# Hybrid encoder, two layers on one core: a bias table stored per query, and a gated product written row-major

## Chip, core and metric

The kernel runs on one core of a Trainium2 chip. The metric is device time in microseconds (us) of one execution, taken as the median of the runs.

## What is computed

Two layers of a bidirectional encoder over 512 tokens of width 1024, all float32. Layer 0 mixes with eight latent-attention heads (MLA) and eight 2-D neighbourhood heads, layer 1 with retention and Hyena; behind each mixer stands a gated convolutional feed-forward block. Every sub-layer is `x = x + rms_norm(f(rms_norm(x)))`. What the change touches:

```python
def neighbourhood_attention(q, k, v, rpb):      # 8 rows x 64 columns of tokens, window 8 x 16
    ...
        row_off = rs + jnp.arange(kh) - r + (NA_WIN_H - 1)
        bias = jnp.transpose(rpb[:, row_off][:, :, col_off], (0, 2, 1, 3))
        s = (jnp.einsum('bchd,bicjhd->bhcij', q_row, k_win).astype(jnp.float32) * scale
             + bias.astype(jnp.float32)[None])
    ...
def conv_ffn(h, w_gate, w_up, conv_w, w_down):
    g = dwconv3(h @ w_gate, conv_w)
    return (jax.nn.gelu(g, approximate=True) * (h @ w_up)) @ w_down
```

## The kernel before

Activations lie transposed: eight tiles of 128 features x 512 tokens. Each float32 product is made of three TensorE products of rounded halves (`mm`, L278: hi x hi, lo x hi, hi x lo, one line each, L280 to L282). Weights come in pieces of 512 KB through SyncE's queue (`load_weight`, L250): DMA into one of two `raw` tiles, ScalarE (ACT) writes `whi` (L259), VectorE (DVE) writes `wlo` (L260), four pairs of them. The order of each engine's instructions is fixed when the program is built: a scheduler with its own costs takes the code's order, with a few priorities (`high_priority`) and pins (`issue_after`).

Layer 0 and its feed-forward block hold the tokens column-major: token position = column x 8 + row. The table of biases `rpb` (8 heads, 15 x 31 offsets) is loaded by eight DMAs of short rows into `rpbraw` (L568 to L570). In `na0` (L626) TensorE multiplies, for each head, a 128 x 128 permutation (`perm`, loaded behind the mask) by a strided view of that head's slice, 384 columns in float32 (L633), which leaves the biases of 128 queries in PSUM; DVE adds three windows of it to the mask (L637). `na1` takes scores and softmax (L655, L658, L666, L671), `na2` transposes and multiplies by the values. The latent projections run between the heads, the MLA heads follow (`ml0` to `ml2`).

In `ffn(l)` (L875) each of 22 steps projects gate (`psA`) and up (`pspj`), convolves and gates; the product (L911) is written over `g` and split into `ahi` and `alo`. `prod(k)` multiplies these by the down weights, 66 matmuls for each of eight output tiles. The block's output is to be row-major (position = row x 64 + column) for layer 1. `boundary` (L339) does this with `perm=True`: the first seven output tiles are multiplied column-major, and the evacuation from PSUM (`evac`, L355 to L364) reads them by the view `rc`. The last one (`late`) is done in two halves of 256 tokens, each 66 matmuls, whose moving operand is read by `rc`: every eighth float, 32 bytes apart. After the first half come its norm (`stats` L292, L297, L299) and, pinned behind 18 matmuls of the second half, `spread` (L316); then `update` on DVE (L395, L396, L334) makes the next block's `h`, and `squares` (L409, L410) runs on ACT and GpSimd (POOL). `proj_halves` is the first work of the next block on it. The feed-forward block of layer 1 has the same code without `rc`.

Of the kernel before, what the change touches and what calls it, by code (L numbers as in the profile page):

```python
# [10 lines left out]
F32 = mybir.dt.float32  # L11
# [5 lines left out]
P = 128  # L17
S = 512
# [25 lines left out]
def shape_constants():  # L44

    c = {}
    tok0 = (np.arange(S) % GR) * GW + np.arange(S) // GR

    def rope(dim):
        inv = np.float32(10000.0) ** (-np.arange(0, dim, 2, dtype=np.float32) / np.float32(dim))  # L50
        ang = np.arange(S, dtype=np.float32)[:, None] * inv.astype(np.float32)[None, :]
        return np.cos(ang).astype(np.float32), np.sin(ang).astype(np.float32)

    co, si = rope(32)
    co, si = co[tok0].T, si[tok0].T
    cc, ss = np.concatenate([co, co]), np.concatenate([-si, si])
    qs = np.float32(MSCALE)
    c["rope0"] = f32(np.stack([np.concatenate([np.full((64, S), qs), cc * qs, ss * qs]),
                               np.concatenate([ss, ss, cc, cc])], 1).reshape(P, 2 * S))
    co, si = rope(128)  # L60
    co, si = co.T, si.T
    c["rope1"] = f32(np.stack([np.concatenate([co, co]), np.concatenate([-si, si])], 1).reshape(P, 2 * S))

    mask = np.zeros((P, 3, 32, GR), np.float32)
    for typ, (q0, k0) in enumerate(((0, 0), (16, 8), (48, 32))):
        for p in range(P):
            col = q0 + p // GR
            st = min(max(col - 8, 0), GW - 16)
            kc = k0 + np.arange(32)
            mask[p, typ, (kc < st) | (kc >= st + 16), :] = -1.0e30  # L70
    perm = np.zeros((P, P), np.float32)
    q = np.arange(P)
    perm[(7 - q % 8) * 16 + 15 - q // 8, q] = 1.0
    c["namask"] = f32(np.concatenate([mask.reshape(P, 3 * 256), perm], 1))

    c["dist"] = f32(np.arange(896)[None, :] - 384 - np.arange(P)[:, None])

    t = np.arange(S, dtype=np.float32) / np.float32(S - 1)
    w = np.float32(2.0 * math.pi) * np.arange(S, dtype=np.float32) / np.float32(S)
    f = np.linspace(1e-4, 15, 16, dtype=np.float32)  # L80
    fw = f[None, :] * w[:, None]
    c["fz"] = f32(np.concatenate([t[:, None], np.cos(fw), -np.sin(fw)], 1).T)
    dl = np.linspace(math.log(1e-2) / 1.5, math.log(1e-2) / 0.3, HC, dtype=np.float32)
    win = np.exp(-t[:, None] * np.abs(dl)[None, :]).astype(np.float32)
    wb = win.copy()
    wb[0] = 0.0
    perm = np.concatenate([np.arange(0, S, 2), np.arange(1, S, 2)])
    c["fwin"] = f32(np.stack([win[perm], wb[perm]]).reshape(2, 4, P, HC).transpose(2, 1, 0, 3).reshape(P, 8 * HC))

    k = np.arange(256)  # L90
    th = (2 * k + 1) * PI / 1024
    mats = []
    for par in (0, 1):
        tt = np.arange(par, S, 2)
        mats += [np.cos(tt[:, None] * th[None, :]), np.sin(tt[:, None] * th[None, :])]
    fwd = f32(np.stack([m.reshape(2, P, 256) for m in mats]))
    inv = f32(np.stack([m.T.reshape(2, P, 256) for m in mats]))
    for name, m in (("dftf", fwd), ("dfti", inv)):
        m = f32(m.transpose(2, 0, 1, 3).reshape(P, 4 * 512))
        hi = rounded(m)  # L100
        c[name] = f32(np.concatenate([hi, m - hi], 1))
    return c
# [13 lines left out]
def lay_out(inp):  # L116
# [75 lines left out]
    ffn(1)  # L192
    a["w"] = f32(np.stack(pieces))

    r = np.transpose(inp["a_rpb"][0], (1, 0, 2))
    a["rpb"] = f32(np.pad(r, ((0, 0), (0, 0), (16, 16))))
    fw = np.zeros((P, 64 + 64 + 64 + 1024), np.float32)
    fw[:33, 0:64] = inp["c_filt_w1"][0]
    fw[:64, 64:128] = inp["c_filt_w2"][0]
# [6 lines left out]
class Body:  # L206
# [132 lines left out]
    def boundary(self, pool, tag, x, prod, gpost, gpre, ns, ftag, perm=False, rin=None):  # L339
# [8 lines left out]
        def evac(k, ps, cs, full):  # L348
            n = cs.stop - cs.start
            f = fs[k][:, cs]  # L350
            src = ps
            if perm and full:
                src, f = rc(ps), v3(f)
            if k == 0:
                nc.scalar.activation(v3(acc[:, cs]) if perm and full else acc[:, cs], src, AF.Square)  # L355
            else:
                sq = new("sq")[:, :n]
                with ExitStack() if full else self.tc.high_priority(HP):
                    nc.scalar.activation(v3(sq) if perm and full else sq, src, AF.Square)
                    if k < KT - 1 or cs.start == 0:  # L360
                        nc.vector.tensor_tensor(acc[:, cs], acc[:, cs], sq, ALU.add)
                    else:
                        lastsq.append(sq)
            nc.scalar.activation(f, src, AF.Copy, scale=self.col(gpost + k))  # L364

        for k in range(KT - ns):
            fs.append(self.X("f", tag=ftag))
# [190 lines left out]

    def mixer0(self, p, h, acc):
        nc = self.nc  # L560
        mask = p.tile([P, 3 * 256 + P], F32, name="namask")
        perm = mask[:, 768:]
        rope = p.tile([P, 2, S], F32, name="rope0")
        rpb = self.I["rpb"]
        big = p.tile([P, 8, 8, 48], F32, tag="big", name="rpbraw")

        def loads():
            for r in range(8):  # L568
                src = bass.AP(rpb.tensor, rpb.offset + r * 504, [[1, 16], [63, 64], [1, 48]])
                nc.sync.dma_start(big[16 * r:16 * r + 16].rearrange("p a b c -> p (a b) c"), src)  # L570
            nc.sync.dma_start(mask, self.I["namask"])
            nc.sync.dma_start(rope, self.I["rope0"].rearrange("p (a b) -> p a b", a=2))
        ebuf = []
        for i in range(4):
# [51 lines left out]
        def na0(hd, _):  # L626
            if hd % 2 == 0:
                q = qk_tile(self.proj(h))
                kn = self.X("kn", tag="xb")
                nc.vector.tensor_tensor(kn, self.proj(h), Rb, ALU.mult)  # L630
                pair[hd // 2] = q, qk_tile(kn)
            ps = self.PS("B")
            nc.tensor.matmul(ps[:, :384], perm, big[:, :, hd].rearrange("p r c -> p c r"), start=True, stop=True)  # L633
            b = p.tile([P, 2, 256], F32, tag="bias", bufs=2, name=self.nm("bias"))
            b = [b[:, 0], b[:, 1], self.X("bias", tag="xb")[:, :256]]
            for t, o in enumerate((128, 64, 0)):
                nc.vector.tensor_tensor(b[t], ps[:, o:o + 256], mask[:, t * 256:t * 256 + 256], ALU.add)  # L637
            return b

        def na1(hd, bias):  # L640
# [234 lines left out]
    def ffn(self, p, x, h, pre, l):  # L875
# [20 lines left out]
        for j in range(FT):  # L896
            if j % 2 == 0:
                next(steps, None)
            gps, ups = pre[2 * j:2 * j + 2] if j < 2 else (self.proj(h, "A"), self.proj(h, "pj"))
            cw = [self.col(C_FC + l * 66 + t * 22 + j) for t in range(3)]  # L900
            t, g = self.X("t"), self.X("g")
            nc.vector.tensor_tensor(t, gps, Rb, ALU.mult)  # L902
            nc.scalar.activation(g, t, AF.Copy, scale=cw[1])
            nc.vector.scalar_tensor_tensor(g[:, sh:], t[:, :S - sh], cw[0], g[:, sh:], ALU.mult, ALU.add)
            nc.vector.scalar_tensor_tensor(g[:, :S - sh], t[:, sh:], cw[2], g[:, :S - sh], ALU.mult, ALU.add)
            if l == 0:
                nc.vector.scalar_tensor_tensor(g[:, 1:8], t[:, 504:511], cw[0], g[:, 1:8], ALU.mult, ALU.add)
                nc.vector.scalar_tensor_tensor(g[:, 504:511], t[:, 1:8], cw[2], g[:, 504:511], ALU.mult, ALU.add)
            nc.scalar.activation(g, g, AF.Gelu_apprx_tanh)

            nc.vector.tensor_tensor(g, ups, g, ALU.mult)  # L911
            hi = p.tile([P, S], F32R, name=f"ahi{l}_{j}")
            lo = p.tile([P, S], F32R, name=f"alo{l}_{j}")
            self.split_to(hi, lo, g)
            a.append((hi, lo))
        rc = lambda t: t.rearrange("p (c r) -> p r c", r=GR)

        def prod(k, late=False):
            w = [self.weight() for _ in range(3)]

            def run(ps, cut):
                for q in range(FT):
                    self.mm(ps, self.wslice(w[q // 8], slice(q % 8 * P, q % 8 * P + P)), (cut(a[q][0]), cut(a[q][1])),
                            q == 0, q == FT - 1)
                    if q in (YQ, FT - 1):
                        yield ps
            if not late:
                return list(run(self.PS("pj"), lambda t: t))[-1]
            if l == 0:
                return lambda cs: run(self.PS("A")[:, :256], lambda t: rc(t)[:, cs.start // GW:cs.stop // GW])  # L930
            return lambda cs: run(self.PS("A")[:, :256], lambda t: t[:, cs])
        return self.boundary(p, "s", x, prod, C_FPOST + 8 * l, C_MPRE + 8 if l == 0 else None, 1, "xa", perm=(l == 0), rin=rcol)


# [338 lines left out]
```

## Time and profile before

| | |
|---|---|
| median of 3 runs | 1348.27 us (1347.58 to 1350.19) |
| profiled execution, its own time | 1350.83 us |
| its span, first to last instruction | 1349.1 us |
| PE (TensorE matmul) busy | 1308.6 us, 97% |
| PEld (weight load) busy | 1079.5 us, 80% |
| DVE / ACT / POOL busy | 812.9 / 571.4 / 149.8 us (60 / 42 / 11%) |
| mean granted clock of TensorE | 0.985 |

Busy times overlap, and matmuls are pipelined: the distance from one start to the next says what one costs, its duration says more than that. An engine's idle time costs only where another one waits for it. The stages lie in the span as follows: neighbourhood heads with latent projections to about 143 us, MLA heads to about 240 us, first feed-forward block from about 310 us, its down products from 536 us, its last output tile from 642.55 us, layer 1 from about 700 us. A clock of 1.0 is TensorE's full one, 0.5 the half.

### The profile page before, as it was taken

To read this page: it belongs to the slowest core of one execution; us is meant where nothing else is said; L and a number is where in the kernel's file an instruction comes from. 1 tells how busy PE (TensorE), PEld (TensorE's weight loads), DVE (VectorE), ACT (ScalarE), POOL (GpSimd) and SP (SyncE) were. 2 spreads that over 40 slices of the span, in tenths; PEclk is the share of its full clock that TensorE was granted. 3 is DMA by queue.
4 is the path that set the end of the run, shared out by engine and by line. 5 is a ranking of instruction groups with operands and counts; after the bars stand their busy time and mean duration, and the time that the engine had idled before them with its cause. 6 is when DMAs were issued, how large, how long until landed. Compare 5 with 4: busy or idle time off the path is not lost. (4 is left out here: it accounts for less than half of the span.)

```text
span 1349.1 us, 16493 instructions
## 1 busy us (share of the span) xinstructions
PE 1308.6 (97%) x6386; PEld 1079.5 (80%) x6386; DVE 812.9 (60%) x1276; ACT 571.4 (42%) x925; POOL 149.8 (11%) x138
## 2 busy tenths in 40 slices
PE   9999899999999999999987999999999999999997
PEld 8777677897877788888986878777988888888886
DVE  7577898388755555222387796785676555552223
ACT  5346699456533333222254333333654333333221
POOL 4011232040001000000050000222120000000002
PEclk9999899999999999999998999999999999999998
DMA  7811001324334323333235222212323333233331
GB/s 194 146 67 63 16 24 57 93 67 132 109 125 141 109 94 94 109 101 103 63 131 181 79 94 93 90 50 66 123 79 111 103 99 94 94 95 108 109 95 63
DMA packets 49146, 130.42 MB, mean 97 GB/s; under 512 B 12875, under 2 KB 15115, under 8 KB 48556
## 3 DMA queue, kind: packets, MB, share of 16 engines
q1 hardware_dynamic: 43452, 116.72, 28.5%
q10 hardware_dynamic: 5040, 8.45, 1.9%
q0 software_dynamic: 576, 4.19, 0.8%
q8 instruction: 50, 0.82, 0.2%
q14 instruction: 28, 0.23, 0.1%
HBM read 123.06 MB, written 6.29 MB: 96 GB/s over the span
## 5 line engine op out<-in xcount | busy, mean ns | idle before, releaser
L259 ACT CAST whi<-raw 128x1024 fp32r<-128x1024 f32 (+1 forms) x200 | 209.1, 1047 | 422.7 <-PE pspj L281 224.1
L260 DVE TENSOR_TENSOR wlo<-raw,whi 128x1024 fp32r<-128x1024 f32 (+1 forms) x200 | 247.3, 1239 | 206.5 <-ACT whi L259 202.4
L280 PE MATMUL pspj<-h,whi 128*128 128x512 f32 (+1 forms) x664 | 252.0, 380 | 0.1
L281 PE MATMUL pspj<-h,whi 128*128 128x512 f32 (+1 forms) x664 | 250.4, 377 | 1.4 <-DVE h L334 1.4
L282 PE MATMUL pspj<-h,wlo 128*128 128x512 f32 (+1 forms) x664 | 249.9, 376 | 0.1
L282 PE MATMUL psA<-h,wlo 128*128 128x512 f32 (+1 forms) x424 | 156.6, 370 | 4.4 <-DVE wlo L260 4.3
L280 PE MATMUL psA<-h,whi 128*128 128x512 f32 (+1 forms) x424 | 157.9, 372 | 0.0
L281 PE MATMUL psA<-h,whi 128*128 128x512 f32 (+1 forms) x424 | 156.1, 368 | 0.0
L281 PEld LDWEIGHTS pspj<-h,whi 128*128 128x128 f32 x664 | 126.1, 190 | 24.4 <-DVE h L334 1.8
L280 PEld LDWEIGHTS pspj<-h,whi 128*128 128x128 f32 x664 | 126.0, 190 | 22.9 <-issue 0.4
L282 PEld LDWEIGHTS pspj<-h,wlo 128*128 128x128 f32 x664 | 125.8, 189 | 22.9 <-DVE wlo L260 0.5
L280 PE MATMUL pspj<-ahi,whi 128*128 128x512 f32 x308 | 121.4, 394 | 0.0
L282 PE MATMUL pspj<-ahi,wlo 128*128 128x512 f32 x308 | 120.7, 392 | 0.0
L281 PE MATMUL pspj<-alo,whi 128*128 128x512 f32 x308 | 119.5, 388 | 0.0
L280 PEld LDWEIGHTS psA<-h,whi 128*128 128x128 f32 x424 | 80.9, 191 | 19.8 <-issue 4.6
L282 PEld LDWEIGHTS psA<-h,wlo 128*128 128x128 f32 x424 | 80.9, 191 | 19.5 <-DVE wlo L260 6.3
L281 PEld LDWEIGHTS psA<-h,whi 128*128 128x128 f32 x424 | 80.9, 191 | 12.6
L299 POOL TENSOR_TENSOR r<-v,mhalf 128x2 f32<-128x2 f32 (+1 forms) x14 | 14.3, 1019 | 636.4 <-DVE v L297 540.7
L902 DVE TENSOR_TENSOR t<-psA,Rb 128x512 f32<-128x512 f32 x40 | 27.6, 691 | 90.5 <-PE psA L282 90.5
L911 DVE TENSOR_TENSOR g<-pspj,g 128x512 f32<-128x512 f32 x40 | 27.6, 691 | 69.8 <-PE pspj L282 63.4
L282 PEld LDWEIGHTS pspj<-ahi,wlo 128*128 128x128 f32 x308 | 57.8, 188 | 13.5
L281 PEld LDWEIGHTS pspj<-alo,whi 128*128 128x128 f32 x308 | 57.8, 188 | 12.9
(351 smaller groups left out, 2265.0 us busy)
## 6 DMA issues: line engine op xcount, KB each, us to landing
raw<-in_w SPq DMA_DIRECT2D x198, 512.0 KB, 3.5
x<-in_xT SPq DMA_DIRECT2D x16, 256.0 KB, 4.6
fc<-in_fwin SPq DMA_DIRECT2D x8, 256.0 KB, 3.4
filt<-fa SPq DMA_DIRECT2D x8, 256.0 KB, 2.0
xspill<-f ACTq DMA_DIRECT2D x8, 256.0 KB, 2.2
sd<-filt ACTq DMA_DIRECT2D x8, 256.0 KB, 3.4
x<-xspill ACTq DMA_DIRECT2D x8, 256.0 KB, 2.9
rpbraw<-in_rpb SPq DMA_DIRECT2D x8, 192.0 KB, 7.9
```

The costliest lines, as they stand in the source:

```text
L259: nc.scalar.copy(hi[:, c], raw[:, c])
L260: nc.vector.tensor_tensor(lo[:, c], raw[:, c], hi[:, c].bitcast(F32), ALU.subtract)
L280: nc.tensor.matmul(ps, stat[0], mov[0], start=start, stop=False)
L281: nc.tensor.matmul(ps, stat[0], mov[1], start=False, stop=False)
L282: self.last_mm = nc.tensor.matmul(ps, stat[1], mov[0], start=False, stop=stop).ins
L299: self.pow = nc.gpsimd.tensor_tensor(r, v, self.mhalf[:, :c], ALU.pow)
L902: nc.vector.tensor_tensor(t, gps, Rb, ALU.mult)
L911: nc.vector.tensor_tensor(g, ups, g, ALU.mult)
```

## The change

Two parts. The bias table is laid out ahead of the run, per query: partition q holds, for each head, the 384 biases that the permutation product made; eight DMAs become four with rows of 3072 bytes, the matmul goes, and DVE adds from SBUF instead of PSUM. In the first feed-forward block DVE writes the gated product row-major into `t` (whose last reader is done), from contiguous reads with writes 256 bytes apart; all down products then read contiguously, and PSUM is evacuated without a permuted view.

```diff
-    perm = np.zeros((P, P), np.float32)
-    q = np.arange(P)
-    perm[(7 - q % 8) * 16 + 15 - q // 8, q] = 1.0
-    c["namask"] = f32(np.concatenate([mask.reshape(P, 3 * 256), perm], 1))
+    c["namask"] = f32(mask.reshape(P, 3 * 256))
...
-    r = np.transpose(inp["a_rpb"][0], (1, 0, 2))
-    a["rpb"] = f32(np.pad(r, ((0, 0), (0, 0), (16, 16))))
+    r = np.pad(inp["a_rpb"][0], ((0, 0), (0, 0), (16, 16)))
+    q = np.arange(P)
+    r = r[:, 7 - (q % GR)[:, None, None] + np.arange(GR)[None, None, :], 15 - (q // GR)[:, None, None] + np.arange(48)[None, :, None]]
+    a["rpb"] = f32(r.transpose(1, 0, 2, 3).reshape(P, MH * 384))
...
-            src = ps
-            if perm and full:
-                src, f = rc(ps), v3(f)
...
-            nc.scalar.activation(f, src, AF.Copy, scale=self.col(gpost + k))
+            nc.scalar.activation(f, ps, AF.Copy, scale=self.col(gpost + k))
...
-        big = p.tile([P, 8, 8, 48], F32, tag="big", name="rpbraw")
+        big = p.tile([P, MH, 384], F32, tag="big", name="rpb")
 
         def loads():
-            for r in range(8):
-                src = bass.AP(rpb.tensor, rpb.offset + r * 504, [[1, 16], [63, 64], [1, 48]])
-                nc.sync.dma_start(big[16 * r:16 * r + 16].rearrange("p a b c -> p (a b) c"), src)
             nc.sync.dma_start(mask, self.I["namask"])
+            for hd in range(0, MH, 2):
+                nc.sync.dma_start(big[:, hd:hd + 2], self.I["rpb"][:, hd * 384:hd * 384 + 768].rearrange("p (a b) -> p a b", a=2))
...
-            ps = self.PS("B")
-            nc.tensor.matmul(ps[:, :384], perm, big[:, :, hd].rearrange("p r c -> p c r"), start=True, stop=True)
...
-                nc.vector.tensor_tensor(b[t], ps[:, o:o + 256], mask[:, t * 256:t * 256 + 256], ALU.add)
+                nc.vector.tensor_tensor(b[t], big[:, hd, o:o + 256], mask[:, t * 256:t * 256 + 256], ALU.add)
...
-            nc.vector.tensor_tensor(g, ups, g, ALU.mult)
+            if l == 0:
+                cr = lambda a: a.rearrange("p (c r) -> p c r", r=GR)
+                nc.vector.tensor_tensor(t.rearrange("p (r c) -> p c r", c=GW), cr(ups), cr(g), ALU.mult)
+                g = t
+            else:
+                nc.vector.tensor_tensor(g, ups, g, ALU.mult)
...
-                return list(run(self.PS("pj"), lambda t: t))[-1]
-            if l == 0:
-                return lambda cs: run(self.PS("A")[:, :256], lambda t: rc(t)[:, cs.start // GW:cs.stop // GW])
-            return lambda cs: run(self.PS("A")[:, :256], lambda t: t[:, cs])
+                return list(run(self.PS("pj"), slice(0, S)))[-1]
+            return lambda cs: run(self.PS("A")[:, :256], cs)
```

The scheduler sets another order in layer 0's mixer; from the MLA heads on the order is the same on every engine. On TensorE, before, the permutation products of heads 0 to 2 stood between the scores of head 1 (`psA_579`) and the next pair's projection (`pspj_535`):

```order
## PE: 6202 rows
187 L280 MATMUL psA_579<-qkh_446,qkh_409 128x256
188 L281 MATMUL psA_579<-qkl_447,qkh_409 128x256
189 L282 MATMUL psA_579<-qkh_446,qkl_410 128x256
190 L633 MATMUL psB_450<-rpbraw,namask 128x384
191 L633 MATMUL psB_457<-rpbraw,namask 128x384
192 L633 MATMUL psB_571<-rpbraw,namask 128x384
193 L280 MATMUL pspj_535<-h_147,whi_380 128x512
194 L281 MATMUL pspj_535<-h_148,whi_380 128x512
195 L282 MATMUL pspj_535<-h_147,wlo_381 128x512
```

With the change one projection of the second pair follows the other directly at this place:

```order
## PE: 6193 rows
181 L280 MATMUL pspj_491<-h_161,whi_315 128x512
182 L281 MATMUL pspj_491<-h_162,whi_315 128x512
183 L282 MATMUL pspj_491<-h_161,wlo_316 128x512
184 L280 MATMUL pspj_527<-h_147,whi_376 128x512
185 L281 MATMUL pspj_527<-h_148,whi_376 128x512
186 L282 MATMUL pspj_527<-h_147,wlo_377 128x512
```

The eight permutation products are gone from TensorE, and head 1's scores stand after the second projection. On DVE, before, the first biases (L637) stood behind the first two pairs' `qkl` and ahead of the first scores (`s_472`):

```order
## DVE: 1260 rows
31 L630 TENSOR_TENSOR kn_413<-pspj_414,Rb_217 128x512
32 L275 TENSOR_TENSOR qkl_447<-kn_413,qkh_446 128x512
33 L275 TENSOR_TENSOR qkl_531<-pspj_499,qkh_530 128x512
34 L637 TENSOR_TENSOR bias_452<-psB_450,namask 128x256 x2
35 L637 TENSOR_TENSOR bias_453<-psB_450,namask 128x256
36 L655 SCALAR_TENSOR_TENSOR s_472<-psA_465,rn,bias_452 128x256
```

With the change four of them (L629) stand ahead of the statistics of the first norm (`v_299`, L295), and behind the last weight split ahead of it:

```order
## DVE: 1260 rows
17 L260 TENSOR_TENSOR wlo_143<-raw_141,whi_142 128x1024
18 L629 TENSOR_TENSOR bias_446<-rpb,namask 128x256 x2
19 L629 TENSOR_TENSOR bias_451<-rpb,namask 128x256 x2
20 L295 TENSOR_SCALAR v_299<-psB_294 128x4
...
39 L275 TENSOR_TENSOR qkl_443<-kn_409,qkh_442 128x512
40 L647 SCALAR_TENSOR_TENSOR s_464<-psA_457,rn,bias_446 128x256 x2
```

The first scores (`s_464`, L647) are then formed before the second pair's `qkl`, and the first biases wait for the mask and the first piece of the table alone.

## Rows read from the trace of the kernel before

**Rows 1.** Page, busy time and share of the span by engine, then instructions.

```profile
PE 1308.6 (97%) x6386; PEld 1079.5 (80%) x6386; DVE 812.9 (60%) x1276; ACT 571.4 (42%) x925; POOL 149.8 (11%) x138
```

**Rows 2.** Busy us (instructions) by stretch; at the end clock, DMA share, GB/s.

```profile
54.00:143.00 89.00, 88.22 (x441) 68.41 (x440) 70.38 (x146) 45.89 (x104) 12.70 (x10) 0.98 0.24 77
143.00:160.00 17.00, 13.48 (x54) 10.23 (x54) 13.78 (x30) 11.33 (x31) 6.17 (x6) 0.70 0.00 1
330.00:535.00 205.00, 205.00 (x873) 161.97 (x872) 122.67 (x187) 76.28 (x95) 10.16 (x8) 1.00 0.35 111
```

**Rows 3.** PE's timeline, permutation products: start, us, what; two passes per product.

```profile
51.02 4.33 PE L633 MATMUL psB<-rpbraw,namask 128*128 128x384 f32 x6
54.57 1.02 PE L280 MATMUL pspj<-h,whi 128*128 128x512 f32 x1
...
76.30 1.52 PE L633 MATMUL psB<-rpbraw,namask 128*128 128x384 f32 x2
77.75 0.38 PE L280 MATMUL psA<-qkh,qkh 64*128 64x256 f32 x1
...
132.94 1.46 PE L633 MATMUL psB<-rpbraw,namask 128*128 128x384 f32 x2
134.23 0.29 PE L677 MATMUL psB<-ident,s 128*128 128x128 f32 x1
```

**Rows 4.** PE's timeline, late products of the first feed-forward block, then its norm.

```profile
642.55 0.38 PE L280 MATMUL psA<-ahi,whi 128*128 128x256 f32 x1
...
658.44 0.40 PE L281 MATMUL psA<-alo,whi 128*128 128x256 f32 x1
658.65 0.74 PE L292 MATMUL psB<-ones,acc 128*128 128x1 f32 x6
...
661.49 0.40 PE L316 MATMUL psC<-ident,r 128*128 128x128 f32 x2
```

**Rows 5.** The same of the second feed-forward block.

```profile
1321.84 0.28 PE L280 MATMUL psA<-ahi,whi 128*128 128x256 f32 x1
...
1330.44 0.28 PE L281 MATMUL psA<-alo,whi 128*128 128x256 f32 x1
1330.71 0.83 PE L292 MATMUL psB<-ones,acc 128*128 128x1 f32 x6
...
1332.66 0.38 PE L316 MATMUL psC<-ident,r 128*128 128x128 f32 x2
```

**Rows 6.** DVE's timeline behind the first late half; in brackets idle before, releaser.

```profile
657.54 0.42 DVE L361 TENSOR_TENSOR acc<-acc,sq 128x256 f32<-128x256 f32 x1 [12.11 <-ACT sq L359]
...
661.92 0.75 DVE L395 TENSOR_TENSOR f<-f,psC 128x256 f32<-128x256 f32 x2 [2.55 <-PE psC L316]
...
665.23 0.48 DVE L334 SCALAR_TENSOR_TENSOR h<-f,cols,h 128x256 fp32r<-128x256 f32 x1
665.63 0.61 DVE L396 TENSOR_TENSOR f<-f,f 128x256 f32<-128x256 f32 x1
...
669.36 1.23 DVE L260 TENSOR_TENSOR wlo<-raw,whi 128x1024 fp32r<-128x1024 f32 x1 [2.06 <-ACT whi L259]
...
673.74 0.16 DVE L297 SCALAR_TENSOR_TENSOR v<-psB,e 128x2 f32<-128x2 f32 x1 [2.76 <-PE psB L292]
...
676.40 1.10 DVE L334 SCALAR_TENSOR_TENSOR h<-f,cols,h 128x256 fp32r<-128x256 f32 x1
...
679.73 0.41 DVE L395 TENSOR_TENSOR f<-f,psC 128x256 f32<-128x256 f32 x1
```

**Rows 7.** POOL's timeline beside it.

```profile
675.02 6.56 POOL L410 TENSOR_TENSOR acc<-acc,f 128x256 f32<-128x256 f32 x6
```

**Rows 8.** PE's longest wait in the next block's first products.

```profile
683.25 0.58 PE L282 MATMUL psA<-h,wlo 128*128 128x256 f32 x1 [1.94 <-DVE wlo L260]
```

**Rows 9.** DVE groups, 330 to 535 us: busy, mean ns | idle before, releasers.

```profile
L911 DVE TENSOR_TENSOR g<-pspj,g 128x512 f32<-128x512 f32 x18 | 12.4, 691 | 29.8 <-PE pspj L282 25.1 <-ACT g L909 4.7
```

**Rows 10.** Page, DMA issues of the table: KB each, us to landing.

```profile
rpbraw<-in_rpb SPq DMA_DIRECT2D x8, 192.0 KB, 7.9
```

More of the change, by code (lines that the diff above doesn't have):

```diff
@@ L350, in evac @@
             f = fs[k][:, cs]
-            src = ps
-            if perm and full:
-                src, f = rc(ps), v3(f)
             if k == 0:
-                nc.scalar.activation(v3(acc[:, cs]) if perm and full else acc[:, cs], src, AF.Square)
+                nc.scalar.activation(acc[:, cs], ps, AF.Square)
             else:
@@ L358, in evac @@
                 with ExitStack() if full else self.tc.high_priority(HP):
-                    nc.scalar.activation(v3(sq) if perm and full else sq, src, AF.Square)
+                    nc.scalar.activation(sq, ps, AF.Square)
                     if k < KT - 1 or cs.start == 0:
@@ L560, in mixer0 @@
         nc = self.nc
-        mask = p.tile([P, 3 * 256 + P], F32, name="namask")
-        perm = mask[:, 768:]
+        mask = p.tile([P, 3 * 256], F32, name="namask")
         rope = p.tile([P, 2, S], F32, name="rope0")
-        rpb = self.I["rpb"]
-        big = p.tile([P, 8, 8, 48], F32, tag="big", name="rpbraw")
+        big = p.tile([P, MH, 384], F32, tag="big", name="rpb")
         def loads():
-            for r in range(8):
-                src = bass.AP(rpb.tensor, rpb.offset + r * 504, [[1, 16], [63, 64], [1, 48]])
-                nc.sync.dma_start(big[16 * r:16 * r + 16].rearrange("p a b c -> p (a b) c"), src)
             nc.sync.dma_start(mask, self.I["namask"])
+            for hd in range(0, MH, 2):
+                nc.sync.dma_start(big[:, hd:hd + 2], self.I["rpb"][:, hd * 384:hd * 384 + 768].rearrange("p (a b) -> p a b", a=2))
             nc.sync.dma_start(rope, self.I["rope0"].rearrange("p (a b) -> p a b", a=2))
@@ L915, in ffn, with run @@
             a.append((hi, lo))
-        rc = lambda t: t.rearrange("p (c r) -> p r c", r=GR)
         def prod(k, late=False):
             w = [self.weight() for _ in range(3)]
-            def run(ps, cut):
+            def run(ps, cs):
                 for q in range(FT):
-                    self.mm(ps, self.wslice(w[q // 8], slice(q % 8 * P, q % 8 * P + P)), (cut(a[q][0]), cut(a[q][1])),
+                    self.mm(ps, self.wslice(w[q // 8], slice(q % 8 * P, q % 8 * P + P)), (a[q][0][:, cs], a[q][1][:, cs]),
                             q == 0, q == FT - 1)
```

## The prediction

> **What bounds the kernel.** I read the page's busy times first. TensorE (PE) is busy for 97% of the span, every other engine for at most 60% [rows 1], so a change counts by what it takes from PE, or by what it makes PE wait for. The stretches come next, because this share is a mean over stages [rows 2]. While the neighbourhood heads run (54 to 143 us), PE is busy for 88.2 of 89 us and DVE for 70.4: PE bounds, with DVE not far behind. From 143 to 160 us, where these heads hand over to the MLA heads, PE works only 13.5 of 17 us and its mean clock is 0.70, that is, 2.4 GHz and 1.2 GHz in turns. In the first feed-forward block (330 to 535 us) PE never stops, and DVE is at 60%. Last I read PE's own timeline at the two places that the diff touches, from one start to the next [rows 3 to 5], and the engines beside the second [rows 6 to 8].
>
> **Part 1, the permutation products.** Heads 0 to 2 have theirs together, from 51.02 us to the next start at 54.57 us: 3.55 us. The other five stand singly; the longest takes 77.75 - 76.30 = 1.45 us, the shortest 134.23 - 132.94 = 1.29 us [rows 3]. With 1.37 us for each of the five, PE loses 3.55 + 5 x 1.37 = 10.4 us of work, in a stage where it has no gaps.
>
> What could take that back is DVE. Its stage of 89 us shrinks to 78.6 us, against 70.4 us of work [rows 2]: 90%. Two things move this figure. Some biases go earlier: without a product to wait for, four stand ahead of the first norm's statistics, where DVE had waited for PE, so the first softmax starts earlier too. The other thing speaks against the change: a bias op had one operand in PSUM and now has both in SBUF. At 676.40 us an L334, all of whose operands are in SBUF, takes 1.10 us while POOL runs its squares (675.02 us, 6.56 us long); without POOL it takes 0.48 us; an L395 with one operand in PSUM keeps its 0.41 us at 679.73 us, still beside POOL [rows 6, 7]. POOL is busy for 12.7 of the 89 us, 14% [rows 2]. If 24 bias ops of 0.42 us (the time of L361 at the same size, from SBUF [rows 6]) meet it that often and grow by 1.10/0.48, DVE does 24 x 0.42 x 0.14 x 1.3 = 1.8 us more. I take 1 us of the 10.4 as given back, because about half of such delays should fall into DVE's remaining gaps: **-9.4 us**. The bounds are 0 (DVE or the hand-over takes all) and -19 us: the 10.4 us, and 8.6 us if the hand-over ran without its 3.5 us of idleness and at full clock (17 us at 0.70 lack 5.1 us).
>
> The Trainium skill, "SBUF — State Buffer", section "SBUF: two separate sides", says that VectorE and GpSimd share one pair of SBUF ports, which a VectorE op with two SBUF inputs and a GpSimd op that reads SBUF take as an exclusive lock for a whole instruction. The trace agrees in kind (0.48 us against 1.10 us). By that rule a bias op could wait for a whole POOL op, 6.56 / 6 = 1.1 us: at 14% of 24 ops some 3.7 us of DVE time, and the sum would be at most 2 us worse.
>
> The table's DMAs I cost at nothing. Eight of 192 KB, 7.9 us to landing [rows 10], become four of the same bytes in long rows, and PE has full work beside them. The four early biases are a new risk: statistics and weight splits are queued behind them on DVE. If the table were late, PE would wait for those splits; but it is now issued earlier in SyncE's queue than before, so I give this nothing, with a bound of one landing, 7.9 us.
>
> **Part 2, the last output tile.** In the first block 73 steps, from 642.55 to 658.44 us, take 15.89 us: 0.218 us for each 256-column matmul [rows 4]. In the second block the same 73, read contiguously, take 8.60 us: 0.118 us [rows 5]. The two halves hold 132 such matmuls, so PE has 132 x 0.100 = 13.2 us less.
>
> The first half's 6.6 us are sure: DVE waits 12.11 us for its result [rows 6], and nothing else is due. Then the chain through statistics and `spread` shortens, because 18 matmuls of the second half are queued ahead of `spread`: from statistics to `spread` it is 2.84 us here [rows 4] and 1.95 us in the second block [rows 5], and the seven ahead of the statistics give 0.7 us more. So DVE's update starts 6.6 + 0.9 + 0.7 = 8.2 us earlier. From there on DVE is what PE waits for: 1.94 us for a weight split that stands in its queue [rows 8]. To keep the whole 13.2 us, DVE has to gain five more. It has idle times of 2.06 and 2.76 us there [rows 6], which end when late matmuls release a weight tile and when they finish the last tile, so both shrink with the matmuls. I take 4 of these 4.8 us: 8.2 + 4.0 = 12.2 us, **-12.2 us**. The bounds are -8.2 us (no idle time shrinks) and -13.2 us.
>
> The first seven output tiles cost the same: they were read contiguously before too. The evacuation only loses its view.
>
> The product itself is the price. L911 takes 0.69 us [rows 9]; its successor writes 256 bytes apart. The nearest row is L396, which reads one operand 32 bytes apart: 0.61 us at 256 elements, against 0.42 us for the contiguous L361 [rows 6]. If a strided write costs what a strided read does, 512 elements take 2 x 0.19 = 0.38 us more, 1.07 us in all; the lower bound is 0.69 us. Over 22 steps that is 8.4 us of DVE work. I cost it at nothing: ahead of L911 DVE is idle for 29.8 us in 18 steps, 1.7 us per step [rows 9], beside a PE without a gap [rows 2], and two `pspj` banks separate the product from the projection that needs its bank.
>
> **The sum.** 1350.83 us (the profiled execution's own time) - 9.4 - 12.2 = 1329.2 us. The median of the runs is 2.56 us below that execution, so the forecast for it is **1326.7 us**.
>
> **The rivals.**
> 1. *The heads give their part back.* DVE at 90% has bursts in which it bounds, and the scheduler has a new order there. For it: DVE's 13.8 of 17 us in the hand-over [rows 2]. Against it: the earlier biases. 1350.83 - 12.2 - 2.56 = 1336.1 us.
> 2. *DVE keeps its pace in the boundary*, as its gaps are filled by other waits: 8.2 us instead of 12.2, so 1330.7 us.
> 3. *The strided product comes onto the path*, by 22 x 0.38 = 8.4 us: 1335.1 us. DVE's idle time speaks against it. The Trainium skill, "Advanced Engine Details and Errata", section "Memory Cachelines", says that accesses to SBUF which go to another 16-byte line each time pay a penalty; this product's writes do that.
> 4. *The hand-over shrinks too*, as PE's idle time and its half clock there depend on an order that is now another one. At half of the 8.6 us: 1322.4 us.
> 5. *The stride is not why the late matmuls are slow.* Everything else is equal in rows 4 and 5, so little speaks for it. Part 1 alone: 1350.83 - 9.4 - 2.56 = 1338.9 us.
> 6. *Slower.* In the heads' stage PE no longer has the filler work of the permutation products; it meets DVE's bursts with gaps, and its clock falls to 1.2 GHz, as at the hand-over (mean 0.70 [rows 2]). A stretch at half clock costs half its length; from 43 us on it eats the 21.6 us. If the stage's 78.6 us of PE work ran at half clock throughout, the time would be 1326.7 + 78.6 = 1405 us. Against it: clock 0.98 in that stage now.
>
> **How the numbers follow.** Forecast 0.60, rival 1 0.14, rival 2 0.10, rival 3 0.04, rival 4 0.06, rival 5 0.03, slower 0.03. Part 1's unknown order is the widest term, so the range runs from 1320 us (rival 4 with most of its gain) to 1337 us (rival 1); rivals 5 and 6 and the far end of 4 stay outside. A measurement of this kernel tells about 0.2% (2.7 us) from no change. All cases but the last are faster by more than that; for mixtures in which most of both parts is lost I leave 0.03 at no change: faster 0.94, same 0.03, slower 0.03.
>
> **What would show it.** Right: the late matmuls of the first block start 0.118 us apart; the interval from the first score product to the MLA heads is about 9 us shorter, with clock near 1; `spread` follows the statistics by about 2 us; the new product takes 0.7 to 1.1 us, and PE has no gap from 330 to 535 us. Wrong: DVE without gaps over tens of us and PE waiting for scores, biases or transposed probabilities (rival 1); PE's waits for `h` and `wlo` behind the late products grown by 4 us or more (rival 2); PE waiting for the release of `pspj` (rival 3).

## The result and the profile after

The changed kernel takes 1325.49 us in the median (1324.58 to 1326.33), against 1349.23 us for the kernel before beside it (1347.58 to 1351.03): ratio 0.9824, 95% interval 0.9807 to 0.9841, that is 23.7 us less. The forecast was 1326.7 us. The profiled execution took 1324.58 us, its span is 1322.8 us.

Page of the kernel after, busy time (answers to [rows 1]) and DMA issues of the table (answers to [rows 10]):

```profile
PE 1280.1 (97%) x6370; PEld 1060.7 (80%) x6370; DVE 820.4 (62%) x1276; ACT 572.2 (43%) x925; POOL 151.2 (11%) x138
...
rpb<-in_rpb SPq DMA_DIRECT2D x4, 384.0 KB, 4.6
```

PE works 28.5 us less and is still the bound. The 16 passes of the eight permutation products are gone, and the table lands in 4.6 us instead of 7.9.

Stretches of the kernel after: the neighbourhood heads, the 17 us of the hand-over (taken 8.76 us earlier, as the MLA heads start at 143.19 instead of 151.95 us), and the first feed-forward block. The columns are those of [rows 2].

```profile
54.00:143.00 89.00, 84.72 (x454) 68.71 (x453) 75.44 (x152) 51.18 (x120) 19.74 (x14) 0.96 0.18 60
134.24:151.24 17.00, 13.24 (x56) 9.63 (x54) 14.07 (x29) 11.94 (x32) 7.79 (x7) 0.70 0.00 0
330.00:535.00 205.00, 205.00 (x872) 161.94 (x871) 121.18 (x175) 75.96 (x94) 10.19 (x8) 1.00 0.36 114
```

The hand-over is as it was: 13.24 of 17 us of PE work at a clock of 0.70, before 13.48 at 0.70. In the feed-forward block PE has no gap, as before. The heads need another cut, from the first score product to the first MLA score. Before first, then after:

```profile
44.24:151.95 107.71, 103.40 (x501) 77.97 (x500) 80.74 (x167) 54.80 (x124) 18.37 (x14) 0.96 0.25 82
```

```profile
47.46:143.19 95.73, 91.45 (x485) 74.09 (x485) 80.65 (x161) 52.88 (x124) 19.74 (x14) 0.96 0.19 61
```

This stretch is 11.98 us shorter, and all of it is busy time of PE: 11.95 us less, and 4.28 us idle where it was 4.31. But it begins 3.22 us later. Here is why. Three timelines of the kernel after, in the lead-in: PE, DVE, ACT; in brackets the idle time before, and what ended it.

```profile
34.77 0.50 PE L280 MATMUL pspj<-h,whi 128*128 128x512 f32 x1 [2.16 <-DVE v L597]
```

```profile
32.82 1.23 DVE L260 TENSOR_TENSOR wlo<-raw,whi 128x1024 fp32r<-128x1024 f32 x1 [3.05 <-ACT whi L259]
33.97 0.75 DVE L597 SCALAR_TENSOR_TENSOR v<-pspj,rcol,v 128x512 fp32r<-128x512 f32 x1
```

```profile
31.74 1.05 ACT L259 CAST whi<-raw 128x1024 fp32r<-128x1024 f32 x1 [2.74 <-DMA raw<-in_w]
32.70 1.26 ACT L596 ACTIVATE v<-pspj,rcol 128x512 fp32r<-128x512 f32 x2
```

ACT's timeline of the kernel before, at the same work:

```profile
29.68 1.31 ACT L602 ACTIVATE v<-pspj,rcol 128x512 fp32r<-128x512 f32 x2 [1.96 <-PE pspj L282]
30.89 1.04 ACT L259 CAST whi<-raw 128x1024 fp32r<-128x1024 f32 x1
```

The values of the first heads leave PSUM by L596 (ACT) and L597 (DVE), and PE waits for a `pspj` bank until they have. In the new order a weight split (L259) stands ahead of the first of them on ACT, and waits 2.74 us for its weights. Before, the first two L602 (the same evacuation) stood ahead of the split at 30.89 us, and PE had no gap here. Of the 3.22 us, 2.16 are this wait. The other 1 us arises earlier: in this execution a tile of `x` landed late (ACT waits 0.84 us for it up to 7.36 us, and not before), and PE's wait for a weight split near 20 us ends at 20.19 us instead of 19.21.

Part 2. PE's timeline of the kernel after, the late products, the norm, and then the waits behind them (answers to [rows 4, 8]):

```profile
631.04 0.28 PE L280 MATMUL psA<-ahi,whi 128*128 128x256 f32 x1
631.16 0.28 PE L281 MATMUL psA<-alo,whi 128*128 128x256 f32 x1
...
639.64 0.28 PE L281 MATMUL psA<-alo,whi 128*128 128x256 f32 x1
639.91 0.83 PE L292 MATMUL psB<-ones,acc 128*128 128x1 f32 x6
...
641.86 0.38 PE L316 MATMUL psC<-ident,r 128*128 128x128 f32 x2
...
653.16 0.39 PE L281 MATMUL pspj<-h,whi 128*128 128x256 f32 x1 [0.47 <-DVE h L334]
...
655.42 0.38 PE L281 MATMUL pspj<-h,whi 128*128 128x256 f32 x1 [0.93 <-DVE h L334]
...
658.81 0.58 PE L282 MATMUL psA<-h,wlo 128*128 128x256 f32 x1 [1.93 <-DVE wlo L260]
```

The 73 steps to 639.64 us take 8.60 us, 0.118 each, exactly as in the second block [rows 5]; before it was 15.89 us. `spread` follows the statistics by 1.95 us, before by 2.84. From the first late product to the first transform product (`dftfhi`) it is 68.92 us before and 55.99 after: 12.93 us less.

DVE's timeline of the kernel after beside it (answers to [rows 6]):

```profile
639.43 0.42 DVE L358 TENSOR_TENSOR acc<-acc,sq 128x256 f32<-128x256 f32 x1 [5.51 <-ACT sq L356]
640.55 0.16 DVE L297 SCALAR_TENSOR_TENSOR v<-psB,e 128x2 f32<-128x2 f32 x1 [0.70 <-PE psB L292]
642.28 0.75 DVE L392 TENSOR_TENSOR f<-f,psC 128x256 f32<-128x256 f32 x2 [1.56 <-PE psC L316]
...
649.31 0.15 DVE L297 SCALAR_TENSOR_TENSOR v<-psB,e 128x2 f32<-128x2 f32 x1
...
651.98 1.12 DVE L334 SCALAR_TENSOR_TENSOR h<-f,cols,h 128x256 fp32r<-128x256 f32 x1
...
673.38 0.53 DVE L334 SCALAR_TENSOR_TENSOR h<-f,cols,h 128x256 fp32r<-128x256 f32 x1 [0.51 <-ACT h L333]
```

The wait for the first late half is 5.51 us instead of 12.11. From 642.28 us on DVE has no idle time until 673 us; the gaps of 2.06 and 2.76 us are gone. The last line is the boundary's last `h`: 42.34 us behind the first late product. In the kernel before it comes 55.18 us behind it, 12.84 us more:

```profile
697.73 0.53 DVE L334 SCALAR_TENSOR_TENSOR h<-f,cols,h 128x256 fp32r<-128x256 f32 x1 [0.51 <-ACT h L333]
```

The 12.93 us end with a product that waits for the transform matrices; these took 8.0 us to land before and 6.8 us after.

The product and the biases, by their lines in the kernel after, and last the biases of the kernel before: minimum, median and maximum in ns, first and last start, and the shape where it is given apart.

```profile
L906 DVE TENSOR_TENSOR t<-pspj,g x20: 1051/1105/1109, 318.1 to 525.5; 128x512 f32<-128x512 f32 x20
...
L629 DVE TENSOR_TENSOR bias<-rpb,namask x24: 409/416/1524, 23.6 to 131.5; 128x256 f32<-128x256 f32 x24
...
L637 DVE TENSOR_TENSOR bias<-psB,namask x24: 414/416/425, 52.6 to 143.1; 128x256 f32<-128x256 f32 x24
```

The strided product takes 1.105 us. A bias takes 0.416 us, the same as with an operand in PSUM; the longest takes 1.524 us, before 0.425.

### The profile page after: what moved, and what is told of

It reads as the page before. It is cut to its first block, busy times and chain, and to the rows that moved or that the text cites. A ratio compares the mean times of both kernels' runs of the same rounds, so it can differ in the third digit from the quotient of the medians.

```text
span 1322.8 us, 16449 instructions
## 1 busy us (share of the span) xinstructions
PE 1280.1 (97%) x6370; PEld 1060.7 (80%) x6370; DVE 820.4 (62%) x1276; ACT 572.2 (43%) x925; POOL 151.2 (11%) x138
## 5 line engine op out<-in xcount | busy, mean ns | idle before, releaser
L259 ACT CAST whi<-raw 128x1024 fp32r<-128x1024 f32 (+1 forms) x200 | 208.9, 1047 | 433.6 <-PE pspj L281 241.4
L280 PEld LDWEIGHTS pspj<-h,whi 128*128 128x128 f32 x664 | 126.0, 190 | 24.7 <-DVE v L597 2.6
L282 PEld LDWEIGHTS pspj<-h,wlo 128*128 128x128 f32 x664 | 126.3, 190 | 22.4
L299 POOL TENSOR_TENSOR r<-v,mhalf 128x2 f32<-128x2 f32 (+1 forms) x14 | 14.3, 1019 | 624.4 <-DVE v L297 543.0
L280 PEld LDWEIGHTS pspj<-ahi,whi 128*128 128x128 f32 x308 | 57.9, 188 | 11.5
```

The source lines that it names most:

```text
L259: nc.scalar.copy(hi[:, c], raw[:, c])
L280: nc.tensor.matmul(ps, stat[0], mov[0], start=start, stop=False)
L282: self.last_mm = nc.tensor.matmul(ps, stat[1], mov[0], start=False, stop=stop).ins
L299: self.pow = nc.gpsimd.tensor_tensor(r, v, self.mhalf[:, :c], ALU.pow)
```

## The experiments

Each of the three sets ran beside the kernel before, on one chip. Ratios are to that kernel's runs.

| kernel | median us (range) | before | ratio, 95% interval |
|---|---|---|---|
| e1, part 1 alone | 1339.58 (1338.76 to 1342.12) | 1347.38 | 0.9942, 0.9928 to 0.9957 |
| e2, part 2 alone | 1338.49 (1336.35 to 1341.41) | 1347.38 | 0.9933, 0.9913 to 0.9952 |
| e4, product written twice | 1326.80 (1325.11 to 1329.28) | 1347.38 | 0.9846, 0.9830 to 0.9862 |
| the whole change again | 1324.61 (1323.87 to 1325.65) | 1347.02 | 0.9841, 0.9828 to 0.9855 |
| e5, whole and earlier values | 1322.49 (1321.03 to 1323.64) | 1347.02 | 0.9825, 0.9812 to 0.9839 |
| e6, packed table for PE | 1343.83 (1343.52 to 1348.00) | 1347.02 | 0.9980, 0.9967 to 0.9993 |
| e3b, other steps | 1346.3 (one run) | 1347.02 | |
| e7, e5 without POOL's additions | 1317.97 (1317.75 to 1318.70) | 1347.76 | 0.9776, 0.9758 to 0.9793 |
| e8, part 1 and earlier values | 1335.74 (1335.30 to 1337.32) | 1347.76 | 0.9910, 0.9894 to 0.9926 |
| e2b, part 2 alone again | 1335.08 (1332.19 to 1337.73) | 1347.76 | 0.9901, 0.9884 to 0.9918 |

### The parts by themselves: e1, e2

e1 has the new table, its layout and DMAs, and the feed-forward block of before; e2 is the reverse. The lines that matter, of e1 and then of e2:

```diff
-            nc.tensor.matmul(ps[:, :384], perm, big[:, :, hd].rearrange("p r c -> p c r"), start=True, stop=True)
...
+                nc.vector.tensor_tensor(b[t], big[:, hd, o:o + 256], mask[:, t * 256:t * 256 + 256], ALU.add)
```

```diff
+            if l == 0:
+                nc.vector.tensor_tensor(t.rearrange("p (r c) -> p c r", c=GW), cr(ups), cr(g), ALU.mult)
+                g = t
...
-                return lambda cs: run(self.PS("A")[:, :256], lambda t: rc(t)[:, cs.start // GW:cs.stop // GW])
+            return lambda cs: run(self.PS("A")[:, :256], cs)
```

> The table part alone; the feed-forward block stays as before. Theory (the two parts save apart from each other, the table by the PE time of its eight permutation products): 9 to 11.5 us under the kernel before, about 1338 to 1340 us, with late products still 0.218 us apart. Rival (most of the whole gain is the rows' part and the heads give theirs back): less than 4 us under, 1345 us or more. What the half clock at 307 us does is open: if it is gone here too, its 1.6 us belong to the table's part.

> The rows' part alone; the table and its permutation products stay as before. Theory (DVE keeps up with the faster last tile): 12 to 14 us under the kernel before, about 1335 to 1337 us, and the two parts' gains add up to the whole change's. Rival (DVE's update keeps its pace): 8 us under, about 1341 us, with DVE's idle times between the weight splits as long as before.

Measured by medians: 7.8 us less for part 1 and 8.9 us for part 2, both less than expected, 16.7 us together. The whole change gives 22.4 us in the next set (21.4 by its ratio), more than the 17 to 20 us expected there. The profiles show where each part acts. With part 1 alone the stretch from the first score to the MLA heads is 95.75 us, as short as after, but it begins only at 50.17 us. PE waits 2.79 us for the values, and its next 14 matmuls run at half clock, 0.435 us apart instead of 0.227, which costs another 2.9 us in this execution (the slowest of e1's four):

```profile
34.67:40.76 6.09, 6.09 (x14) 4.78 (x15) 3.15 (x4) 1.27 (x2) 0.00 (x0) 0.51 0.53 172
```

The boundary, from the first late product to the first transform product, is 0.8 us shorter. With part 2 alone the heads are unchanged (107.8 us) and the boundary is 12.03 us shorter. So the parts act in separate places, and e8 and e2b below ask whether they add up.

### The product's price: e4

```diff
-                nc.vector.tensor_tensor(t.rearrange("p (r c) -> p c r", c=GW), cr(ups), cr(g), ALU.mult)
+                for _ in range(2):
+                    nc.vector.tensor_tensor(t.rearrange("p (r c) -> p c r", c=GW), cr(ups), cr(g), ALU.mult)
```

> The changed kernel with the strided gated product of each of the first block's 22 steps done twice, the same values into the same tile: 22 x 1.1 = 24 us more work for DVE there, and 1.1 us more before each split. Theory (the product lies wholly beside TensorE's work): the time of the changed kernel, 1325.5 us within 3 us. Rival (it is partly on the path): later by up to 24 us, 1349 us, with PE waiting for a pspj bank.

The stretch of the feed-forward block with the product written twice:

```profile
330.00:535.00 205.00, 205.00 (x872) 161.93 (x871) 142.39 (x198) 77.27 (x96) 10.16 (x8) 1.00 0.37 113
```

DVE does 21 us more than after, and PE still has no gap in 205 us. The median is 20.6 us under the kernel before on its chip, that of the whole change 22.4 and 23.7 in its two sets; by ratio the intervals overlap. The profiles are closer: from the MLA heads to the first late product it is 489.2 us here and 488.8 in "whole". So 22 further strided products, 24 us of DVE work, cost nothing that stands out of the scatter, and the 22 x 0.41 us by which the first ones became longer are hidden too. Rival 3 falls.

### The step in memory: e3b

The kernel before, with the first block's products written at other steps and read back at them by the late products:

```diff
-            nc.vector.tensor_tensor(g, ups, g, ALU.mult)
+            if l == 0:
+                n = 2 if j < 11 else 4
+                cr = lambda a: a.rearrange("p (s c) -> p s c", s=n)
+                nc.vector.tensor_tensor(t.rearrange("p (c s) -> p s c", s=n), cr(ups), cr(g), ALU.mult)
+                g = t
...
+                two = lambda t: t.rearrange("p (c s) -> p s c", s=2)[:, 0:1]
+                four = lambda t: t.rearrange("p (c s) -> p s c", s=4)[:, 0:2]
```

> The kernel before, but the first half of the last output tile reads its moving operand at a step of 2 floats (8 bytes) and the second half at 4 floats (16 bytes), instead of 8; and the first eleven gated products are written at a step of 2 floats, the other eleven at 4. The block thus multiplies and writes permuted tokens; its sizes are the same. Theory (what costs is that each read or write goes to another 16-byte line; by the Trainium skill, Advanced Engine Details and Errata, section Memory Cachelines): step 2 is free, 0.118 us between starts and 0.69 us per product, step 4 costs as much as step 8, 0.218 us and 1.10 us. Rival A (any step costs): 0.218 us and 1.10 us at both. Rival B (the cost grows with the step): in between, such as 0.13 and 0.16 us.

DVE's timeline of e3b: the last product of the steps that write 8 bytes apart, and the first that writes 16 bytes apart.

```profile
408.12 0.69 DVE L914 TENSOR_TENSOR t<-pspj,g 128x512 f32<-128x512 f32 x1 [1.72 <-PE pspj L282]
...
419.00 1.09 DVE L914 TENSOR_TENSOR t<-pspj,g 128x512 f32<-128x512 f32 x1 [1.72 <-PE pspj L282]
```

PE's timeline of e3b: first late half, read 8 bytes apart (to 639.19 us), and second, read 16 bytes apart.

```profile
638.52 0.39 PE L280 MATMUL psA<-ahi,whi 128*128 128x256 f32 x1
638.73 0.41 PE L281 MATMUL psA<-alo,whi 128*128 128x256 f32 x1
638.96 0.41 PE L282 MATMUL psA<-ahi,wlo 128*128 128x256 f32 x1
639.19 0.41 PE L280 MATMUL psA<-ahi,whi 128*128 128x256 f32 x1
...
664.31 0.42 PE L280 MATMUL psA<-ahi,whi 128*128 128x256 f32 x1
...
667.09 0.42 PE L280 MATMUL psA<-ahi,whi 128*128 128x256 f32 x1
```

The two engines differ. For DVE's writes, 8 bytes apart is free (0.69 us, as in [rows 9]), 16 bytes apart costs 1.09 us and 256 bytes 1.105: the whole price is there at 16 bytes and is the same at 256. All eleven products of either step say so (0.67 to 0.70 us, 1.08 to 1.09 us). That agrees with the Trainium skill, "Advanced Engine Details and Errata", section "Memory Cachelines", on lines of 16 bytes. For PE's reads the price is there at the smallest step: 0.227 us at 8 bytes, (667.09 - 664.31) / 12 = 0.232 us at 16, 0.218 us at 32 [rows 4], against 0.118 contiguous [rows 5]. A boundary of 16 bytes does not explain that; at these three steps it mattered to PE only whether the row is contiguous. The clock was 1.00 at both rows of starts.

### The permutation products without their stride: e6

The kernel before, keeping the products, with the table stored so that PE reads each head's 384 columns contiguously, by eight DMAs, one per head:

```diff
-            nc.tensor.matmul(ps[:, :384], perm, big[:, :, hd].rearrange("p r c -> p c r"), start=True, stop=True)
+            nc.tensor.matmul(ps[:, :384], perm, big[:, hd], start=True, stop=True)
```

> The kernel before with its permutation products kept, but with the table stored so that their moving operand is contiguous instead of 1536 bytes from one float to the next; eight DMAs, as before, now of long rows. Theory (a part of these products' price is the step): by the contiguous float32 products of L991, 1.06 us for two passes of 512 columns, 384 columns should take 0.8 us instead of 1.2 to 1.45, so 3 to 4 us under the kernel before, 1344 us. Rival (at the slower rate of float32 the step is hidden): 1.2 to 1.45 us as before and the same time.

PE's timeline of e6 at one such product (compare [rows 3]):

```profile
61.56 0.81 PE L635 MATMUL psB<-rpbraw,namask 128*128 128x384 f32 x2
62.30 0.38 PE L284 MATMUL psA<-qkh,qkh 64*128 64x256 f32 x1
```

0.74 us instead of 1.29 to 1.45: here too the stride nearly doubled the time. Eight products at 0.74 us are 5.9 us, so some 4.5 of the 10.4 us of part 1 were the stride, the rest the product itself. Heads and hand-over are 100.31 us instead of 107.71, but not for the same work: two of the products stand ahead of the first score here, which comes 4.52 us later. The median is 3.2 us less (0.9 to 4.4 by the interval).

### The wait in the lead-in: e5 and e8

The weights' look-ahead is one piece shorter while the values are projected, so the order on ACT puts the values ahead of the weight split again:

```diff
-        while len(self.wq) < AHEAD + 1 and self.wi < self.I["w"].shape[0]:
+        while len(self.wq) < self.ahead + 1 and self.wi < self.I["w"].shape[0]:
...
+        self.ahead = AHEAD - 1
         pss = self.proj_tok(h, {7: loads, 5: lambda: self.stats([acc], D, out=self.rcol),
...
             nv.append(v)
+        self.ahead = AHEAD
```

e5 has this on top of the whole change, "whole" is the change once more beside it, and e8 has it on top of part 1 alone.

> The whole change again, beside the kernel before on this chip, because the parts alone measured 7.8 and 8.9 us and the whole 23.7 us. Theory (the parts add up, and medians of four runs scatter): 17 to 20 us under the kernel before. Rival (the two parts help each other): 22 to 25 us under.

> The changed kernel, with one weight fewer loaded ahead during the first projection, so that DVE's first two value splits (L597 of the changed kernel) stand ahead of the third weight split, not behind it. Theory (the new wait of 2.2 us of TensorE at 34.8 us on a value split comes from that weight split, which waits for its DMA): the wait goes, 2 us under the whole change in the same call. Rival (the wait only moves to the weight itself): no change.

> Part 1 alone (the table per query) together with the earlier values, the feed-forward block as before. Part 1 alone measured 7.8 us less than the kernel before, less than the forecast 9.4. Theory (the heads gave their whole 10.4 us and more; the wait for the values in the lead-in took some 2 us back): without that wait 9.5 to 12 us less than the kernel before, the first score product near 44 us. Rival (the heads themselves give part back): 7 to 9 us less.

e5 is the fastest version that computes everything: 1322.49 us against 1324.61 for the whole change on the same chip, and the two ranges do not overlap. Its PE has no wait for the values, and its first score starts at 43.95 us, that of "whole" at 46.06 with a wait of 1.76 us for `v`. e8 gains 12.0 us where e1 gained 7.8, its first score at 44.24 us, to the hundredth where it is before. Its heads:

```profile
44.24:139.66 95.42, 91.41 (x485) 74.04 (x485) 80.26 (x160) 52.74 (x123) 19.73 (x14) 0.97 0.19 61
```

So part 1 is worth 12 us by medians (10.0 to 14.3 by the interval) where its new order does not make the values late; the shortfall lies in the lead-in and not in the heads. Both kernels keep the four early biases, so these were not what delayed the values.

### Do the parts add up: e2b

The kernel of e2 once more.

> Part 2 alone (the row-major product) once more, in five rounds and on the same chip as part 1 with the earlier values. Alone it had measured 8.9 us less than the kernel before, with an interval of 6.5 to 11.7, while its profile showed the boundary 12.0 us shorter. If the parts add up, it is 11 to 13 us less, and with part 1 and the earlier values 22 to 25 us, as both together measured 23.6. If one part takes from the other, about 9 us less again and a sum under 21.

12.7 us less. With e8's 12.0 that is 24.7, and e5, which is both, gives 24.5 (1347.02 - 1322.49). They add up, as far as intervals of some 4 us can tell. e2's 8.9 stays the odd value; its interval ends at 11.7 us, and its own profile shows the boundary 12.03 us shorter. Its runs had a lower clock: 0.985 in the mean of the four, 0.9875 in that of e2b's six. By the runs of the kernel before in e2b's set (from 1346.28 us at 0.990 to 1353.47 us at 0.983) that is, as an estimate, some 2 of the 3.4 us between the two medians. Why the clock was lower, and the rest, stay open.

### What bounds the boundary now: e7

e7 is e5 without POOL's additions of squares behind the first feed-forward block:

```diff
-                    nc.gpsimd.tensor_tensor(v(acc2[:, cs]), v(acc2[:, cs]), own(k, cs), ALU.add)
+                    if not perm:
+                        nc.gpsimd.tensor_tensor(v(acc2[:, cs]), v(acc2[:, cs]), own(k, cs), ALU.add)
```

> The changed kernel with the earlier values, and without GpSimd's additions of squares in the boundary behind the first feed-forward block: the next norm is then made from one tile of squares instead of eight, so layer 1 gets another scale; the amount of its work is the same. In the changed kernel DVE works there without a gap from 642 to 673 us, and its operations with all operands in SBUF take 1.1 us beside GpSimd instead of 0.48 us. Theory (DVE sets the pace of this boundary since the late products became short, and GpSimd slows it): some ten operations beside GpSimd are up to 0.6 us shorter, so the stretch from the first late product to the first transform product is 3 to 6 us shorter than in the kernel with the earlier values (56 us), and the time 1317 to 1320 us against its 1322.5. Rival (PE's 48 us of work there, its lower clock and the transform matrices' DMA set the pace): no difference above 1 us.

DVE's groups between the first late product and the first transform product: e5 first, then e7. Busy us and mean ns of one, then idle time before.

```profile
L394 DVE TENSOR_TENSOR f<-f,f 128x256 f32<-128x256 f32 x16 | 13.1, 837 | 0.0
L335 DVE SCALAR_TENSOR_TENSOR h<-f,cols,h 128x256 fp32r<-128x256 f32 x16 | 11.0, 706 | 0.5 <-ACT h L334 0.5
...
L393 DVE TENSOR_TENSOR f<-f,psB 128x256 f32<-128x256 f32 x8 | 3.1, 416 | 0.0
```

```profile
L394 DVE TENSOR_TENSOR f<-f,f 128x256 f32<-128x256 f32 x16 | 10.2, 662 | 0.0
L335 DVE SCALAR_TENSOR_TENSOR h<-f,cols,h 128x256 fp32r<-128x256 f32 x16 | 7.3, 478 | 0.5 <-ACT h L334 0.5
...
L393 DVE TENSOR_TENSOR f<-f,psB 128x256 f32<-128x256 f32 x8 | 3.1, 414 | 0.0
```

The operations with all operands in SBUF become 2.9 and 3.7 us shorter in all; those that read PSUM do not change. The time falls to 1317.97 us: 29.8 us under the kernel before, where e5 stood 24.5 under it, so 5.3 us. The stretch from the first late product to the first transform product, of e5, e7 and e4 in turn:

```profile
628.13:683.03 54.90, 50.27 (x377) 47.41 (x376) 40.02 (x73) 28.32 (x51) 20.20 (x20) 0.97 0.38 133
627.85:678.23 50.38, 48.33 (x377) 45.90 (x376) 33.70 (x73) 28.11 (x51) 4.88 (x6) 1.00 0.41 143
631.68:686.53 54.85, 48.90 (x377) 46.02 (x375) 38.44 (x72) 28.33 (x51) 20.10 (x20) 1.00 0.40 140
```

It is 50.38 us instead of 54.90, and of PE's waits of 0.47, 0.97 and 1.94 us there one of 0.77 is left. DVE's last `h` comes 36.05 us behind the first late product instead of 42.33. Part of the 4.5 us is clock: 0.97 in e5, 1.00 in e7. e4, which has e5's boundary, ran it at 1.00 too, and PE reaches the next norm (`psB<-ones,acc`) 46.89 us behind the first late product in e5, 45.46 in e4 and 42.36 in e7: 3.1 us are left at equal clock. Whether e7's clock is higher because the waits are shorter, no run shows. So the theory holds in the main: since the late products are short, DVE sets the pace there, and POOL slows DVE. The lengths of DVE's operations agree in kind with the Trainium skill, "SBUF — State Buffer", section "SBUF: two separate sides", as the prediction tells it. An edit that adds these squares elsewhere was not tried.

## Why the prediction was right

The forecast of 1326.7 us stood 1.2 us from the result. Its steps were not all right.

**PE's work in part 1** was 10.4 us by the products' own rows. The heads' stretch became 12.0 us shorter, in PE's busy time alone; in seven executions with the new table it is 95.4 to 95.8 us. Most of the 1.6 us that are over belongs to the profiled execution of before, whose clock stood at half from 78.7 to 82.1 us. e2b has the heads of before, no half clock there, and 106.21 us:

```profile
44.36:150.57 106.21, 102.02 (x501) 76.56 (x500) 80.49 (x167) 55.03 (x124) 18.36 (x14) 0.98 0.28 85
```

Against that the new table takes 10.4 to 10.8 us from the heads, as the term said. One reading of [rows 3] was short: at 54.57 us the last pass still runs, and the matmul that starts there has its own successor 0.87 us later instead of 0.227, so the first three products cost some 4.2 us and not 3.55, and the eight 11.0 us.

```profile
55.44 0.40 PE L281 MATMUL pspj<-h,whi 128*128 128x512 f32 x1
```

**What DVE gives back** was the wrong step. I took 1 us of the 10.4 as lost in the heads, to biases that meet POOL. They do meet it (the longest 1.524 us), but the median is 0.416 us and the stretch lost nothing: PE's idle time there is the same to 0.03 us. What was lost, 2 us, went in the lead-in, to a wait that I had looked for only on DVE, as a late table. The table was early; the order on ACT was what had changed. Of the forecast's -9.4, the profile shows 12.0 - 3.2 = 8.8 us at the MLA heads. The 1 us given back in the heads was taken for nothing, the 2 us of the lead-in were left out: two errors of opposite sign, and that they partly cancel is luck.

**The hand-over** stayed as I assumed (13.24 of 17 us, clock 0.70); rival 4 did not come.

**Part 2** held step by step: 0.118 us per matmul, `spread` 1.95 us after the statistics. The term was -12.2; the profile shows -12.93 on PE and -12.84 on DVE, e2b's median -12.7. I took 4 of DVE's 4.8 us of idle time; all of it went, which with the 8.2 us makes 13.0. PE's three waits behind the late products kept their length (the longest 1.93 us, before 1.94 [rows 8]), so rival 2 falls. Rival 5 falls by the 0.118 us and by e2.

**The product** was estimated at 1.07 us and takes 1.105. It is hidden, as the idle time of [rows 9] said, and e4 shows that twice its work would be hidden too.

**The clock** did not fall further in the heads (0.96 in both profiles), so rival 6 falls. It fell ahead of them in e1's profile, right behind PE's wait for the values.

**The sum** of the two profiles, 1350.83 - 1324.58 = 26.3 us, is larger than that of the medians, 23.7: the profiled execution of before was 1.6 us over its own median now, and that of after 0.9 us under. Half-clock stretches are part of such differences. Beside the one at 78.7 us, one stood at 307 to 311 us before (0.57); after, the same work, in the same order, runs at 1.00, and there the changed kernel's lead grows by 1.6 us. But the profiles of e2, e2b, e3b and e6, which all keep the permutation products, show no half clock there either, so it is that execution's and no gain of the change.

## What to carry to other kernels

Look at the step of every moving operand: a matmul that reads its columns with gaps took nearly twice as long here, with each gap tried, while a strided write on an engine with idle time hid the same permutation for nothing. When an edit lets a scheduler set a new order, follow every engine's queue in the stretch ahead of the edit as well, because a split that waits for a transfer can come to stand in front of an evacuation. When one engine's work in a stage goes, ask which engine is now without gaps there, and what makes its instructions long.

## What the hardware showed beyond that

- PE pays for a step at once and nearly the same for the three tried (0.227, 0.232 and 0.218 us at 8, 16 and 32 bytes; 0.118 contiguous), DVE's write not yet at 8 bytes (0.69 us; 1.09 at 16, 1.105 at 256).
- The first late half of e3b ran at a granted clock of 1.00 throughout, as that of before did, so these prices are not the clock's. Nor does half the clock raise them: in e3b's second half matmuls with a step of 16 bytes start 0.234 us apart from 658.95 to 661.52 us, at 0.50, where contiguous ones double (0.435 us instead of 0.227 for 512 columns in e1).

```profile
658.58:661.52 2.94, 2.94 (x14) 2.94 (x13) 2.48 (x6) 1.41 (x3) 0.00 (x0) 0.50 0.00 0
```

- A wait of PE can cost its length again: behind e1's 2.79 us the clock fell to half, which took another 2.9 us. Behind the waits of 2.16 us (after), 1.79 us (e4) and 1.76 us ("whole") at the same place it stayed at 1.00.
- The heads' stretch has the same length at different clocks: 95.73 us at 0.96 with 4.28 us of PE idle (after), 95.77 us at 0.99 with 5.28 us (e5). What PE gained by the clock it waited longer for DVE's probabilities (`s`) at the hand-over, 2.99 us instead of 2.23, so there PE's clock does not set the pace.

```profile
43.95:139.72 95.77, 90.49 (x485) 73.66 (x485) 80.66 (x161) 52.89 (x124) 19.75 (x14) 0.99 0.20 61
```
